# The beginning of a second mixer re-ordered: ScalarE roots, staggered norms, values projected tile by tile, weight splits on GpSimd, the last modulation third moved

## The chip, the cores and the metric

One core of a Trainium2 chip runs the kernel as one program. The metric is the device time of one execution in microseconds (us), the median of several. TensorE (PE) does the matrix products and the transposes, VectorE (DVE), ScalarE (ACT) and GpSimd (POOL) the rest; SyncE (SP) issues most of the transfers. A "slot" is a buffer on the chip that successive tiles of one kind share.

## The reference, cut to what matters

The model has two layers over 256 context and 256 latent tokens (512 tokens, four tiles of 128, width 1024). Each layer is a token mixer and then a mixture of experts, each followed by a residual and a layer norm:

```
for l in range(2):
    sh1, sc1, g1, sh2, sc2, g2 = split(silu(c) @ w_ada[l] + b_ada[l], 6)   # for latents and for context
    h = layer_norm(x) * (1 + sc1) + sh1
    p = h @ w_in[l]          # columns: query down, key/value down, mLSTM q, k, values, output gate, gates, merge gates
    y = (g_a * mla(p) + g_b * mlstm(p)) @ w_out[l]
    x = layer_norm(ALPHA * x + g1 * y, ln1_g[l], ln1_b[l])
    x = layer_norm(ALPHA * x + g2 * hier_moe(modulate(x, sh2, sc2)), ln2_g[l], ln2_b[l])
```

`layer_norm` subtracts the mean and multiplies by `rsqrt(var + 1e-6)`. The mLSTM is a chunked recurrence with gates from 16 columns of `p`; the kernel computes it as masked products over whole tiles, for which the gates' running sums and running maxima are needed first. In the second layer only the latent tokens go on to an output.

## The kernel before

All products are in float32. To keep accuracy with the faster form of float32, an operand is split in a rounded part and a rest: ScalarE copies the rounded part (`split_sb`, L176), and `sub` (L160) subtracts it, on GpSimd every third time and else on VectorE; `mm3` (L192) then does three products for one (L196 to L198).

A planner orders each engine's instructions before the run, by the program's order and its own estimate of when each is ready; on the chip each engine then takes its queue in that order. `issue_after(x)` in the new code puts what a block issues behind the instruction `x` on the engine of `x`. `keep_in_program_order` fixes a transfer in its queue. Generators are woven by hand: `weave(main, steps, fills)` runs one step of `main` and then its share of each filling generator.

The weights of the mixer come through four slots of 128x2048, handed out in halves (`w`, L118); `load_cols` (L438) loads columns of a matrix, `wsplit` (L453) splits them. The shared pools `st` (12 tiles of 128x512), `pm` (4) and `u` (34 in the second layer) hold the rest.

The end of the first layer's experts (`moe`, L1296): the last two pairs of experts are combined into the rows `X[t]` of each tile (`combine`, L1467: a product, L1478 and L1481 on VectorE). Then, tile by tile, come the norm with gains (`stats`, L1487: a square with a sum on ScalarE, L1492, then an inverse root by three Newton steps of VectorE instructions on 128x1, L144 to L154; then L1574 and L1581) and the statistics of the next layer's first norm (again `stats`). After all four tiles the middle third of the second layer's modulation, `ada(1, 1, True)`, is drained: 16 loads of w_ada and 64 matrix instructions (L382). A call `ada(l, g)` does one third g of the six modulation rows of layer l.

The second mixer's begin (`mixer`, L467): `vkr`, the 256 columns for the position key, the gates and half of the key/value down projection, are loaded and split first. Then, for each tile t and each half g of its width, ScalarE writes the normalised half `xn` (L493), TensorE transposes it (L499), ScalarE and VectorE scale and shift (L508, L510), and the result is split into `hTh` and `hTl` (L511, L512). With each half goes a step of `ada(1, 2)`, the last modulation third. Then `tm` (L549) projects each tile on `vkr` (L571), `gates` (L787) makes the gates' sums, maxima and transposes on VectorE while keys and queries are projected (`cm`, L559), the four heads' value columns are loaded, split and projected by `mv_cols` (L594), and the mLSTM is woven with the latent projections (L684). In the first layer, two modulation thirds (1 and 2 of that layer) are woven there as well.

Of the kernel before, what the change touches and what calls it, by code (L numbers as in the profile page):

```python
# [83 lines left out]
class Kern:  # L84
# [77 lines left out]
    def split_sb(self, src, name="s", weights=False):  # L162
# [14 lines left out]
        self.sub(view(lo), src, view(hi).bitcast(F32))  # L177
# [135 lines left out]
    def setup(self):  # L313
# [25 lines left out]
        self.ada_d = [self.dp.tile([2, 6 * D], F32, name=f"ada{l}") for l in range(L)]  # L339
        self.zeros = self.cp.tile([128, 1], F32, name="zeros")  # L340
# [14 lines left out]
    def ada(self, l, g, late=False):  # L355
# [5 lines left out]
        def bias():  # L361
            bt = self.pm(name="bada") if late else (self.u(name="bada") if first else self.w("bada")[:, 0:512])
            for c in range(4):
                a = g * 2048 + c * 512
                (nc.gpsimd if first else nc.sync).dma_start(out=bt[32 * c:32 * c + 32],
                                                            in_=I["b_ada"][l, a:a + 512].partition_broadcast(32))
            return bt
# [85 lines left out]
    def wsplit(self, vs, cols=None):  # L453

        res = []
        for v in vs:
# [10 lines left out]
    def mixer(self, l):  # L467
# [10 lines left out]
        hl = mp.tile([128, 8, 512], F32R, tag="hT", name="hTl", bufs=2)  # L478
        if l == 0:
            xT, xs = [], {}  # L480
            ada0 = self.ada(0, 0)
            next(ada0)
        else:

            vkr = self.load_cols(win, 512, 160, (2208, 96))
            wkr = self.wsplit(vkr)
            ada0 = self.ada(1, 2)
        for t in range(NT):
            r, nb = self.nlx[t] if l else self.ln_scale(self.X[t])
            ts = slice(t * 128, t * 128 + 128)  # L490
            for g in range(2):
                xn = (self.u if l else self.st)(name="xn")
                nc.scalar.activation(xn, self.X[t][:, g * 512:g * 512 + 512], AF.Identity, scale=r, bias=nb)  # L493
# [3 lines left out]
                p = self.ps("t")  # L497
                for k in range(4):
                    nc.tensor.transpose(p[:, k * 128:(k + 1) * 128], xn[:, k * 128:(k + 1) * 128], self.ident)  # L499
# [21 lines left out]
        run(ada0)  # L521
        if l == 0:
# [26 lines left out]
        def tm(v, toks, ws=None):  # L549

            ws = ws or self.wsplit(v)
            n = v[0].shape[2]
            for t in toks:
                p = self.ps("g")
                s = slice(t * 128, t * 128 + 128)
                self.mm3(p[:, 0:n], [(hh[:, k, s], hl[:, k, s], ws[k][0], ws[k][1]) for k in range(8)])
                yield t, p

# [9 lines left out]
        krg = self.sm([128, NT, 48], "krg", bufs=1)  # L568
        kd2 = [self.u(name="kd") for i in range(2)]
        kd = {t: kd2[t // 2][:, (t % 2) * 256:(t % 2) * 256 + 256] for t in range(NT)}  # L570
        for t, p in enumerate(pkr) if l == 0 else tm(vkr, range(NT), wkr):  # L571
            nc.scalar.activation(kd[t][:, 128:256], p[:, 0:128], AF.Copy)
            nc.vector.tensor_copy(krg[:, t], p[:, 128:176])
# [14 lines left out]
        V1 = [mp.tile([128, self.UW], F32, tag="u", name="v1", bufs=self.NU).rearrange("p (a b) -> p a b", a=NT)  # L588
              for h in range(4)]
        tpo = [self.u(name="tpo").rearrange("p (a b) -> p a b", a=4) for h in range(4)]  # L590
        for h in range(4):
            nc.gpsimd.memset(V1[h][:, :, 128:129], 1.0)

        def mv_cols():  # L594
            for c in range(2):
                v = self.load_cols(win, 1184 + c * 256, 256)
                for t, p in tm(v, range(NT)):
                    for i in range(2):
                        nc.scalar.activation(V1[2 * c + i][:, t, 0:128], p[:, i * 128:i * 128 + 128], AF.Copy)  # L599
                    yield  # L600
# [70 lines left out]
        for _ in range(4):  # L671
            next(fill)
# [935 lines left out]
```

## Time and profile before

| | |
|---|---|
| median of 3 runs | 1428.43 us (1427.02 to 1432.36) |
| the profiled execution's own time | 1431.51 us |
| its span, first to last instruction | 1429.4 us |
| busy in the span: TensorE | 1294.4 us (91%) |
| busy: VectorE, ScalarE, GpSimd | 794.9, 451.2, 377.7 us |
| mean granted TensorE clock | 0.947 of full speed |
| read from HBM | 344.62 MB |

Busy time is the time in which an engine has an instruction in work. Matrix products overlap, and their ends are modelled, so that a TensorE which is busy all the time need not be at its peak. The mean over the span mixes stages with different limits, so the seam between the layers has to be read by itself.

### The profile page before, as it was taken

The page shows a single profiled execution, that of the slowest core. Times are in us where ns is not written, and L with a number is a line of the kernel's source. Part 1 is how long each engine was busy: PE and PEld are TensorE (multiplying, and loading weights), DVE is VectorE, ACT ScalarE, POOL GpSimd, SP SyncE. Part 2 cuts the span into 40 slices and gives each one's busy share as a digit, 9 for nine tenths or more (in the row PEclk, how much of TensorE's full clock was granted, in tenths as well). Part 3 has the DMA queues.
Part 4 walks back from the last instruction along what each step waited for, and adds up shares of the span by engine and source line. Part 5 has one row for each costly group of instructions (what it writes and reads, how often), then busy time and mean ns, then how long its engine had stood idle before and what let it go on. Part 6 is the DMA issues. An engine that isn't in the chain of part 4 may idle for free. (4 is left out here: it accounts for less than half of the span.)

```text
span 1429.4 us, 19667 instructions
## 1 busy us (share of the span) xinstructions
PE 1294.4 (91%) x6839; PEld 834.8 (58%) x6839; DVE 794.9 (56%) x2189; ACT 451.2 (32%) x998; POOL 377.7 (26%) x385
## 2 busy tenths in 40 slices
PE   5899999999999828999999959999999749999995
PEld 1788867776776623444454517898878634444342
DVE  3745777553236945555554486478775863343325
ACT  3534344443340102111121137356545212121121
POOL 1310114100343302444343212112524401232222
PEclk9999999999999858989999989999999959999998
DMA  9633464211247567979999968321444768999994
GB/s 326 207 114 131 145 214 140 82 30 59 89 177 269 168 256 250 403 264 409 408 407 409 403 211 278 96 81 39 152 143 132 237 250 329 408 408 406 407 409 158
DMA packets 145970, 339.64 MB, mean 238 GB/s; under 512 B 21552, under 2 KB 67792, under 8 KB 145856
## 3 DMA queue, kind: packets, MB, share of 16 engines
q1 hardware_dynamic: 137184, 322.61, 61.7%
q0 software_dynamic: 6224, 10.31, 2.1%
q10 hardware_dynamic: 2448, 5.31, 1.0%
q8 instruction: 59, 0.97, 0.3%
q14 instruction: 55, 0.45, 0.1%
HBM read 344.62 MB, written 4.29 MB: 244 GB/s over the span
## 5 line engine op out<-in xcount | busy, mean ns | idle before, releaser
L1438 PE MATMUL ps_g<-we,xs 128*64 128x512 f32 x992 | 243.7, 617 | 6.6 <-DMA we<-in_w_e_up 4.2
L1438 PEld LDWEIGHTS ps_g<-we,xs 128*64 128x64 f32 x992 | 76.3, 141 | 148.2 <-issue 141.6
L160 POOL TENSOR_TENSOR wsl<-wc,wsh 128x512 fp32r<-128x512 f32 x54 | 72.5, 1346 | 321.7 <-ACT wsh L176 284.1
L1484 POOL TENSOR_TENSOR X<-X,acc 128x512 f32<-128x512 f32 x96 | 125.2, 1327 | 109.8 <-DVE acc L1478 109.7
L160 DVE TENSOR_TENSOR wsl<-wc,wsh 128x512 fp32r<-128x512 f32 x108 | 84.5, 786 | 98.3 <-ACT wsh L176 87.0
L176 ACT ACTIVATE wsh<-wc 128x512 fp32r<-128x512 f32 x162 | 99.0, 628 | 118.6 <-PE ps_g L197 81.1
L1442 DVE SCALAR_TENSOR_TENSOR si<-si,ws,ps_g 128x256 f32<-128x256 f32 (+1 forms) x33 | 15.8, 480 | 211.4 <-ACT si L1441 211.4
L1461 PE MATMUL ps_a<-we,hidT 128*64 128x512 f32 x496 | 125.3, 595 | 2.1 <-DMA we<-in_w_e_down 1.9
L1394 POOL DMA_INDIRECT xr<-h2d,ti x33 | 34.9, 1057 | 315.2 <-PE ps_t L1406 207.2
L196 PE MATMUL ps_g<-hTh,wsh 128*128 128x512 f32 (+1 forms) x320 | 112.4, 351 | 2.0 <-ACT tg L639 2.0
L197 PE MATMUL ps_g<-hTl,wsh 128*128 128x512 f32 (+1 forms) x320 | 111.1, 347 | 0.0
L198 PE MATMUL ps_g<-hTh,wsl 128*128 128x512 f32 (+1 forms) x320 | 110.6, 346 | 0.0
L196 PE MATMUL ps_g<-wsh,hTh 128*128 128x256 f32 x368 | 105.5, 289 | 2.5 <-ACT v L599 2.4
L197 PE MATMUL ps_g<-wsl,hTh 128*128 128x256 f32 x368 | 104.2, 284 | 0.0
L198 PE MATMUL ps_g<-wsh,hTl 128*128 128x256 f32 x368 | 103.7, 283 | 0.0
L382 PE MATMUL ps_d<-wada,sT 128*32 128x512 f32 x380 | 70.3, 645 | 29.5 <-DMA wada<-in_w_ada 29.4
L1478 DVE TENSOR_TENSOR acc<-ps_d,g 128x512 f32<-128x512 f32 x108 | 74.1, 689 | 38.0 <-PE ps_d L1476 21.9
L1441 ACT ACTIVATE si<-ps_g 128x256 f32<-128x256 f32 (+1 forms) x33 | 12.7, 384 | 245.7 <-PE ps_g L1438 179.0
L1475 PE MATMUL ps_d<-yh,pmr 128*128 128x512 f32 (+1 forms) x200 | 83.7, 419 | 0.4 <-DVE acc L1478 0.2
L1461 PEld LDWEIGHTS ps_a<-we,hidT 128*64 128x64 f32 x496 | 38.6, 137 | 76.1 <-issue 62.8
L1476 PE MATMUL ps_d<-yl,pmr 128*128 128x512 f32 (+1 forms) x200 | 80.2, 403 | 0.9 <-DVE yl L190 0.9
L196 PEld LDWEIGHTS ps_g<-wsh,hTh 128*128 128x128 f32 x368 | 69.6, 190 | 9.2 <-ACT v L599 2.6
(420 smaller groups left out, 2710.3 us busy)
## 6 DMA issues: line engine op xcount, KB each, us to landing
we<-in_w_e_gate SPq DMA_DIRECT2D x124, 512.0 KB
we<-in_w_e_up SPq DMA_DIRECT2D x124, 512.0 KB
we<-in_w_e_down SPq DMA_DIRECT2D x124, 512.0 KB
wada<-in_w_ada SPq DMA_DIRECT2D x95, 512.0 KB
wc<-in_w_in SPq DMA_DIRECT2D x63, 512.0 KB
wc<-in_w_out SPq DMA_DIRECT2D x16, 512.0 KB
wc<-in_w_bo_mla SPq DMA_DIRECT2D x8, 512.0 KB
wc<-in_w_bo_mlstm SPq DMA_DIRECT2D x6, 512.0 KB
```

The costliest lines, as they stand in the source:

```text
L160: eng.tensor_tensor(out=out, in0=a, in1=b, op=OP.subtract)
L176: self.nc.scalar.activation(view(hi), src, AF.Copy)
L196: self.nc.tensor.matmul(out, lhsT=ah, rhs=bh, start=(i == 0), stop=False)
L197: self.nc.tensor.matmul(out, lhsT=ah, rhs=bl, start=False, stop=False)
L198: self.nc.tensor.matmul(out, lhsT=al, rhs=bh, start=False, stop=(i == n - 1))
L382: nc.tensor.matmul(ps[32 * c:32 * c + 32], lhsT=self.sT[:, kb], rhs=wt[c // 2][:, (c % 2) * 512:(c % 2) * 512 + 512], start=(kb == 0), sto ...
L1438: nc.tensor.matmul(p[64 * e:64 * e + 64], lhsT=xs[:, k, 64 * e:64 * e + 64], rhs=W[e, k], start=(k == 0), stop=(k == 7))
L1461: nc.tensor.matmul(p[64 * e:64 * e + 64], lhsT=hT_[:, c, 64 * e:64 * e + 64], rhs=W[e, c, h], start=(c == 0), stop=(c == 1))
L1475: nc.tensor.matmul(p, lhsT=lt, rhs=yh[h][0:m], start=(j == 0), stop=False)
L1476: nc.tensor.matmul(p, lhsT=lt, rhs=yl[h][0:m], start=False, stop=(j == len(parts) - 1))
L1478: nc.vector.tensor_tensor(out=a, in0=p, in1=g2[t // 2][h], op=OP.mult)
L1484: nc.gpsimd.tensor_tensor(out=X, in0=X, in1=a, op=OP.add)
```

## The change

Six things change. The first and the last touch the norms of both layers, the others only the seam between the first layer's experts and the second mixer.

1. `stats` takes the root on ScalarE (`AF.Sqrt` with the scale 1/D and a constant column for epsilon), then VectorE's reciprocal and one Newton step, in place of three Newton steps from an integer guess. It serves the second norm of both layers and the statistics of the next first norm.
2. The norm of a tile becomes a generator with three parts: combination and mean; first norm and the next mean; second statistics. After the experts only the parts (0, 1, 0, 2, 1, 3) by tile are run, the rest at the beginning of the mixer, where each tile starts as soon as its norm is there.
3. In the second layer each tile is projected on `vkr` and on both value matrices right after its start (`from_start`). The values' eight splits are subtracted on GpSimd alone, in tiles from `u`, and their ScalarE copies stand behind tile 0's last copy; the splits of `vkr` stand behind tile 0's last normalised half.
4. Both halves of a tile are normalised and transposed before the first is modulated, and `xn` lies in `st` instead of `u`.
5. The last modulation third, `ada(1, 2)`, is woven with the mLSTM instead.
6. The bias rows of the late modulation third are issued by GpSimd instead of SyncE, and the sums of the norm lie in another small pool.

```diff
-    def split_sb(self, src, name="s", weights=False):
+    def split_sb(self, src, name="s", weights=False, pool=False):
...
         self.nc.scalar.activation(view(hi), src, AF.Copy)
-        self.sub(view(lo), src, view(hi).bitcast(F32))
+        if pool:
+            self.nc.gpsimd.tensor_tensor(out=view(lo), in0=src, in1=view(hi).bitcast(F32), op=OP.subtract)
+        else:
+            self.sub(view(lo), src, view(hi).bitcast(F32))
...
-                (nc.gpsimd if first else nc.sync).dma_start(out=bt[32 * c:32 * c + 32],
+                (nc.gpsimd if late or first else nc.sync).dma_start(out=bt[32 * c:32 * c + 32],
...
-                h, lo = self.split_sb(v[:, k:k + m], "ws", True)
+                h, lo = self.split_sb(v[:, k:k + m], "ws", not far, far)
...
             vkr = self.load_cols(win, 512, 160, (2208, 96))
-            wkr = self.wsplit(vkr)
-            ada0 = self.ada(1, 2)
-        for t in range(NT):
+            krg, kd, kd2 = start_tiles()
+            vv = [self.load_cols(win, 1184 + c * 256, 256) for c in range(2)]
+        def start(t, between=None):
...
-                xn = (self.u if l else self.st)(name="xn")
-                nc.scalar.activation(xn, self.X[t][:, g * 512:g * 512 + 512], AF.Identity, scale=r, bias=nb)
+                xn = self.st(name="xn")
+                done = nc.scalar.activation(xn, self.X[t][:, g * 512:g * 512 + 512], AF.Identity, scale=r, bias=nb)
...
+            if between:
+                with tc.issue_after(done.ins):
+                    between()
+            for g, p in enumerate(pts):
...
-                nc.scalar.activation(oh, h, AF.Copy)
+                done = nc.scalar.activation(oh, h, AF.Copy)
                 self.sub(ol, h, oh.bitcast(F32))
-                next(ada0)
+            return done
+
+        def from_start(t):
+            kr_out(t, next(tm(vkr, [t], wkr))[1])
+            for c in range(2):
+                mv_out(c, t, next(tm(vv[c], [t], wmv[c]))[1])
...
+            wkr, wmv = [], []
+            norm(0)
+            done = start(0, lambda: wkr.extend(self.wsplit(vkr)))
+            norm(2, 1)
+            with tc.issue_after(done.ins):
+                wmv.extend(self.wsplit(v, None, True) for v in vv)
+            start(1)
+            from_start(0)
+            norm(3, 2)
+            start(2)
+            from_start(1)
+            norm(3)
+            start(3)
+            from_start(2)
+            from_start(3)
...
         def mv_cols():
-            for c in range(2):
+            for c in range(0 if l else 2):
...
-        fill2 = self.chain(*[self.ada(0, g) for g in (1, 2)]) if l == 0 else iter(())
+        fill2 = self.chain(*[self.ada(0, g) for g in (1, 2)]) if l == 0 else self.ada(1, 2)
...
-        self.weave(mlstm, 10, [(fill, 32 if last else 34), (fill2, 16)])
+        self.weave(mlstm, 10, [(fill, 32 if last else 34), (fill2, 8 if last else 16)])
...
-            nc.scalar.activation(xrs[xi[0] % 3], X, AF.Square, bias=nm, accum_out=q)
-            nc.vector.tensor_scalar(v, q, 0.5 / D, 0.5 * eps, op0=OP.mult, op1=OP.add)
-            self.newton(r, v, a)
+            junk = self.cp.tile([128, 1024], BF16, tag="st", name="junk", bufs=self.NST)
+            nc.scalar.activation(junk, X, AF.Square, bias=nm, accum_out=q)
+            nc.scalar.activation(r0, q, AF.Sqrt, scale=1.0 / D, bias=self.eps[eps])
+            nc.vector.tensor_scalar(v, q, -0.5 / D, -0.5 * eps, op0=OP.mult, op1=OP.add)
+            nc.vector.reciprocal(r0, r0)
+            nc.vector.tensor_scalar(a, r0, v, r0, op0=OP.mult, op1=OP.mult)
+            nc.vector.scalar_tensor_tensor(r, a, 1.5, r0, op0=OP.add, op1=OP.mult)
...
+        self.norms = {t: norm(t) for t in QT}
+        for t in (2, 2, 3, 3) if last else (0, 1, 0, 2, 1, 3):
+            next(self.norms[t])
```

`kr_out` and `mv_out` write a tile's projection out of TensorE's banks with the instructions that stood at L572, L573 and L599. `start_tiles` hands out the tiles for this, the value tiles with their column of ones among them, earlier than before.

## Rows read from the trace of the kernel before

**Rows 1.** Table by stretches: us, busy per engine (instructions), granted clock, DMA share, GB/s.

```profile
831.50:859.10 27.60, 12.07 (x40) 1.75 (x40) 21.75 (x76) 11.16 (x20) 4.36 (x4) 0.75 0.61 223
...
906.40:916.10 9.70, 7.36 (x49) 7.36 (x50) 4.43 (x12) 3.62 (x10) 1.29 (x1) 0.82 0.14 47
```

**Rows 2.** Groups by form, TensorE, 820 to 932: count, busy, mean ns, idle.

```profile
L196 PE MATMUL ps_g<-wsh,hTh 128*128 128x256 f32 x105 | 30.8, 293 | 2.5 <-ACT v L599 2.4 <-ACT hTh L511 0.2
...
L196 PE MATMUL ps_g<-hTh,wsh 128*128 128x512 f32 x16 | 6.3, 396 | 0.0
...
L196 PE MATMUL ps_g<-hTh,wsh 128*128 128x256 f32 x16 | 4.6, 287 | 0.0
```

**Rows 3.** Timeline, TensorE, 824 to 869: start, us, engine, line, count [idle before].

```profile
824.37 7.07 PE L382 MATMUL ps_d<-wada,sT 128*32 128x512 f32 x64
...
868.00 0.28 PE L196 MATMUL ps_g<-wsh,hTh 128*128 128x256 f32 x1
...
868.12 0.29 PE L197 MATMUL ps_g<-wsl,hTh 128*128 128x256 f32 x1
```

**Rows 4.** Waits of TensorE, 820 to 932: total us, times, longest.

```profile
PE ps_d L382 <- DMA wada<-in_w_ada: 15.0, 5, 11.0
...
PE ps_g L196 <- ACT v L599: 2.4, 1, 2.4
```

**Rows 5.** Waits of all engines, 831 to 880.

```profile
PEld ps_d L382 <- DMA wada<-in_w_ada: 26.6, 12, 11.9
...
ACT xr L1492 <- DVE ln_mv L1584: 23.4, 4, 7.8
```

**Rows 6.** Waits of the sync queue, 790 to 930.

```profile
SPq L378 <- DVE wsl L160: 15.4, 1, 15.4
```

**Rows 7.** Timeline, ScalarE, 822 to 885.

```profile
823.34 1.15 ACT L1492 ACTIVATE xr<-X,ln_mv 128x1024 f32<-128x1024 f32 x1 [6.39 <-DVE ln_mv L1572]
...
841.81 2.17 ACT L176 ACTIVATE wsh<-wc 128x512 fp32r<-128x512 f32 x4
...
858.28 4.32 ACT L493 ACTIVATE xn<-X,ln_nb,ln_r 128x512 f32<-128x512 f32 x6
```

**Rows 8.** Timeline, VectorE, 822 to 885.

```profile
828.72 0.15 DVE L147 TENSOR_SCALAR ln_r<-ln_v 128x1 int32<-128x1 int32 x1
...
830.90 1.28 DVE L1581 SCALAR_TENSOR_TENSOR X<-X,ln_r,ln 128x1024 f32<-128x1024 f32 x1
...
844.41 1.77 DVE L160 TENSOR_TENSOR wsl<-wc,wsh 128x512 fp32r<-128x512 f32 x1
...
846.47 0.68 DVE L160 TENSOR_TENSOR wsl<-wc,wsh 128x512 fp32r<-128x512 f32 x1
```

**Rows 9.** Timeline, ScalarE, 885 to 960.

```profile
885.87 1.28 ACT L800 ACT_TABLE_LOAD   x1
...
917.46 0.20 ACT L857 ACTIVATE em<-ps_t 128x32 f32<-128x32 f32 x1 [0.31 <-DVE uT L856]
```

**Rows 10.** Timeline, GpSimd, 822 to 940.

```profile
842.52 3.11 POOL L160 TENSOR_TENSOR wsl<-wc,wsh 128x512 fp32r<-128x512 f32 x2 [0.78 <-ACT wsh L176]
```

**Rows 11.** Timeline, VectorE, 884 to 935.

```profile
885.89 0.21 DVE L573 COPY krg<-ps_g 128x48 f32<-128x48 f32 x1 [0.18 <-ACT kd L572]
...
917.24 0.19 DVE L856 COPY uT<-ps_t 128x32 f32<-128x32 f32 x1
```

**Rows 12.** Instructions of L382, first layer's mLSTM: duration min/median/max, first and last start.

```profile
L382 PE MATMUL ps_d<-wada,sT x112: 592/592/617, 112.3 to 219.7; 128*32 128x512 f32 x112
```

**Rows 13.** Table by stretches, first layer's mLSTM.

```profile
100.00:200.00 100.00, 100.00 (x705) 77.52 (x704) 65.71 (x241) 45.44 (x140) 12.45 (x9) 1.00 0.49 166
```

**Rows 14.** Timeline, VectorE, the kernel's end.

```profile
1424.61 1.41 DVE L1578 SCALAR_TENSOR_TENSOR X<-X,ln_r,ln 128x512 f32<-128x512 f32 x2
```

**Rows 15.** Table by stretches, before and in the last experts' stage.

```profile
1160.00:1180.00 20.00, 7.18 (x28) 4.12 (x30) 15.32 (x86) 4.61 (x7) 3.01 (x3) 0.50 0.49 190
...
1200.00:1220.00 20.00, 19.70 (x97) 8.45 (x97) 5.81 (x18) 4.64 (x10) 4.49 (x4) 1.00 1.03 408
```

More of the change, by code (lines that the diff above doesn't have):

```diff
@@ L339, in setup @@
         self.ada_d = [self.dp.tile([2, 6 * D], F32, name=f"ada{l}") for l in range(L)]
+        self.eps = {}
+        for e in (EPS, EPS / ALPHA ** 2):
+            self.eps[e] = self.cp.tile([128, 1], F32, name=f"eps{len(self.eps)}")
+            nc.gpsimd.memset(self.eps[e], e)
         self.zeros = self.cp.tile([128, 1], F32, name="zeros")
@@ L510, in mixer, with norm @@
                         nc.vector.tensor_scalar(h[:, k], pv[:, k], sc, sh, op0=OP.mult, op1=OP.add)
-                nc.scalar.activation(oh, h, AF.Copy)
+                done = nc.scalar.activation(oh, h, AF.Copy)
                 self.sub(ol, h, oh.bitcast(F32))
-                next(ada0)
+            return done
[3 more added lines that the diff above has]
+                mv_out(c, t, next(tm(vv[c], [t], wmv[c]))[1])
+        if l == 0:
+            for t in range(NT):
+                start(t)
+        else:
+            def norm(*ts):
+                for t in ts:
+                    next(self.norms[t])
[14 more added lines that the diff above has]
+            from_start(3)
         if l == 0:
@@ L520, in mixer @@
                 nc.scalar.activation(xT[k], p, AF.Copy)
-        run(ada0)
-        if l == 0:
+            run(ada0)
             tc.keep_in_program_order(nc.sync.dma_start(out=self.cst, in_=I["cst"][:, C_CAPF:]))
@@ L565, in cm @@
             return p
[L568 to L573, printed above, removed]
+        if l == 0:
+            krg, kd, kd2 = start_tiles()
+            for t, p in enumerate(pkr):
+                kr_out(t, p)
         gen = self.gates(l, krg[:, :, 32:48])
@@ L587, in mixer @@
                     next(gen)
-        V1 = [mp.tile([128, self.UW], F32, tag="u", name="v1", bufs=self.NU).rearrange("p (a b) -> p a b", a=NT)
-              for h in range(4)]
         tpo = [self.u(name="tpo").rearrange("p (a b) -> p a b", a=4) for h in range(4)]
-        for h in range(4):
-            nc.gpsimd.memset(V1[h][:, :, 128:129], 1.0)
         def mv_cols():
-            for c in range(2):
+            for c in range(0 if l else 2):
                 v = self.load_cols(win, 1184 + c * 256, 256)
                 for t, p in tm(v, range(NT)):
-                    for i in range(2):
-                        nc.scalar.activation(V1[2 * c + i][:, t, 0:128], p[:, i * 128:i * 128 + 128], AF.Copy)
+                    mv_out(c, t, p)
                     yield
@@ L671, in mixer @@
         for _ in range(4):
-            next(fill)
+            next(fill, None)
         gates = next(gen)
@@ L1564, in moe, with norm @@
         self.drain(comb)
-        sums = {t: sm([128, 3], "sum", bufs=n) for t in QT}
+        sums = {t: self.ss_tile([128, 2, 6], "st")[:, 0] for t in QT}
         comb = combine(done, sums)
-        for t in QT:
+        def norm(t):
             for h in range(2):
@@ L1587, in moe @@
             self.nlx[t] = (r, nb)
+            yield
+        self.norms = {t: norm(t) for t in QT}
+        for t in (2, 2, 3, 3) if last else (0, 1, 0, 2, 1, 3):
+            next(self.norms[t])
         if not last:
```

50 lines of the change are left out of this document (34 added, 16 removed).

## The prediction, made before the changed kernel had run

> **What bounds the kernel now.** The kernel's two layers are a mixer and a mixture of experts each, and the change sits at the seam between the first layer's experts and the second mixer, plus the last norm of the kernel. So I read the views of that seam. First the table by stretches, for TensorE [rows 1]: it is busy for 12.07 of the 27.6 us from 831.5, where the experts' last product and the middle modulation third are through, and even that at a clock of 0.75. I take the seam to end at 932, with the second mLSTM in full swing: 100.5 us. How much of that is work? The groups by form hold 105 records of the 128x256 product's first line; its two sister lines have 104 each, and the same form with the operands the other way round has 16 in each of three lines, 361 in all; the 128x512 form has three groups of 16 [rows 2]. Back to back a 128x256 product starts 0.12 us after the one before [rows 3], so 361 are 43 us; 48 of twice the width, at twice that (an estimate), 11.5 us; the last modulation third is 64 instructions, which took 7.07 us when its sister third ran undisturbed [rows 3]; some 48 transposes and small products at about 0.12 us, 6 us. That is 67 to 68 us of work. **TensorE loses 33 us here**, and this is all that a rearrangement of the seam can win.
>
> Next, who makes it wait. TensorE's own list names the modulation's weights for 15.0 us, one wait of 11.0 in it, and the evacuation of a value projection for 2.4 [rows 4]; on the weight loader's own count the same cause makes 26.6 us [rows 5]. But the load was late only because its slot was: the sync queue stood 15.4 us before that load, until VectorE's last split of the first w_in columns (key and gate columns) [rows 6]. And that split was late because ScalarE takes its instructions in order: it waited 23.4 us for the norms' means [rows 5], did the splits at 841.81 and the first normalised tile only at 858.28, behind the last tile's squares [rows 7], though tile 0's normalised rows were there when the instruction at 830.90 had run [rows 8] plus one more statistic. Tile 0 waits for tile 3; that is the seam's chain.
>
> **The change part by part.** The profiled execution took 1431.51 us, a span of 1429.4 and 2.1 around it; the median of the three runs is 1428.43, 3.1 less. The terms below come from that execution and are microseconds saved against its own time; the result is then carried to the median.
>
> *Roots on ScalarE.* Eight small VectorE steps per statistic become four, and one root. Tile 0's first Newton chain runs from 828.72 to 830.90 with other work between [rows 8], about 0.3 a step, so three dependent steps are 0.9 and the root 0.20, as the small exponential is [rows 9]: a saving of about 1 per statistic on the chain. Against it stands a function table, 1.28 for the one load that this trace shows beside an exponential [rows 9]; squares, copies and identities ran on the tables of either neighbour without a load. One load at the seam, one at the end. The Trainium skill (ScalarE: Activation LUTs, What ACT_TABLE_LOAD costs) puts a switch to another set at 2.66 us with its drain; the row shows the load's 1.28 and no drain, and by the page the two places would cost 2.8 more together, 1419.3.
>
> *Staggered norms.* Tile 0 no longer waits for tile 3. From its first square at 823.34, 1.25 long with the read [rows 7]: load 1.28, root and steps 1.1, the affine row 1.28, mean 0.15, giving 828.4; the second square, root, steps and shift 2.5, giving 830.9; two normalised halves at 0.72 (six in 4.32 [rows 7]), giving 832.3; transposes, modulation, copy and subtract, about 3.4 by their chain's pieces, giving 836. VectorE is full then, with evictions and tile 1's norm before this in its queue: up to 5 later. I take 839: TensorE waits 7 (4.5 to 9.5) from 831.5, less its transposes.
>
> *Clock after the wait.* In the stretch 906.4 to 916.1, after a wait of 2.4, the granted clock was 0.82 of the full 2.4 GHz, and in 831.5 to 859.1, with its long waits, 0.75, so part of the time at 1.2 [rows 1]. 0.18 of 9.7 is 1.7; two such dips are 3.5 (1.7 to 6.9, the latter 0.25 of 27.6).
>
> *Values per tile, splits on GpSimd.* A tile now feeds three projections of 24 products, 2.9 each. The two value weights need eight splits on GpSimd, 3.11 for two [rows 10], so 12.4 after the first copy, and four of them, 6.2, before any value product. They queue behind tile 0, so from about 837 to 850. Tile 0's and 1's key projections (5.8) and tile 0's first value projection (2.9) fill in; the rest, 3.7, is waited out: I take 4 (0 to 9.5, where only tile 0's key projection is there to fill).
>
> *VectorE beside GpSimd.* The same subtract took 1.77 while GpSimd's ran and 0.68 after [rows 8, 10], 1.09 more. Eight times that is 8.7 on VectorE, which has some 20 of work left then; TensorE is 7 or so behind it with queued projections, so most is hidden. I take 2 (0 to 8.7). The Trainium skill (SBUF — State Buffer, Who interferes with whom) calls this an exclusive lock: a VectorE instruction with two SBUF inputs waits out a GpSimd one that reads SBUF. The trace agrees, with 1.77 against 0.68; by the rule in full, with every split costing VectorE its whole length, the term would be 12.4 and the time 1426.9, which the first rival below takes in.
>
> *The gates' cover.* From the last key and gate columns at 885.89 to the transposed gates at 917.24 are 31 us [rows 11], a VectorE chain that TensorE fills with query, key and value projections; the values are now used up before. What is left: one tile's values 5.8, keys 11.5, queries 5.8, together 23. Unless the latent projections are pulled ahead, 8 is uncovered: I take 4 (0 to 8).
>
> *The last modulation third in the mLSTM.* Its 64 instructions count as work in either place. The first layer weaves two thirds through its own mLSTM, 112 instructions from 112.3 to 219.7 [rows 12], and there TensorE was busy 100 of 100 us [rows 13]. I take 2 for slots and queue (0 to 15.0, what TensorE waited for these loads at the seam [rows 4]). At the seam the sync queue now carries only the six halves of the first projections; key columns behind them wait for a slot that the first splits free, long before need. The bias rows moved to GpSimd's queue stand ahead of its splits and cost under 1.5, hidden behind tile 0.
>
> **Sum.** 33 less (7 + 3.5 + 4 + 2 + 4 + 2 = 22.5) is 10.5. At the end of the kernel VectorE ends its last norm at 1426.0 (1424.61 and 1.41) [rows 14]; two tiles spare eight steps, some 3, and pay one table load: 1.5 (0.3 to 2.5). Together 12. It should carry through: 1160 to 1180, before the last experts, the weight queues are half idle (0.49), and the 408 GB/s stream that bounds the rest is full only later [rows 15]; its slots come free with the mixer, so it starts earlier with it. Result: 1431.5 - 12 = 1419.5 us for an execution like the profiled one, and 3.1 less for the median, **1416.5 us**.
>
> **The rivals.**
> *GpSimd's splits set the seam's pace.* Value projections wait 9.5 in place of 4 and VectorE pays 8.7 in place of 2: 12.2 less saved, 1428.7. For it: GpSimd's row and the doubled subtract. Against: VectorE's slack.
> *The gates' chain lies bare.* 8 in place of 4: 1420.5; for it the wait of 2.4 there already [rows 4].
> *Slower: the mLSTM waits for the woven third.* The sync queue is in order; one load before an occupied slot holds every projection's weights behind it. At the seam such waits came to 26.6 on the loader [rows 5]. That in place of 2 gives 1441; past 21 of waiting the result is more than 0.5% slower, past 14 the gain is gone. For it: 15.4 of queue wait for one slot [rows 6]. Against: the first layer's full TensorE [rows 13].
> *It does not carry.* If the expert weights' stream has its own start, only the end's 1.5 stays: 1427. Against: the half-idle queues [rows 15].
>
> **How the numbers follow.** Forecast 0.57, GpSimd 0.14, gates 0.10, slower 0.09, not carried 0.10. A measurement here tells 0.5%, 7.1 us, from no change. The forecast's own range, its waits all small or two of them large, is 1406 to 1422. The 8-in-10 range reaches over the gates and to GpSimd and the case that does not carry: 1406 to 1430. Faster by over 0.5% (under 1421.3) holds most of the forecast and half of the gates' case: 0.60; within, 0.28; slower, 0.12.
>
> **What would show it.** Tile 0's normalised halves near 833 and its first key product near 839; no modulation products between 831 and 880; one table load of 1.28 before the first root; GpSimd's eight subtracts in a row; last key columns near 870 to 875 and the mLSTM's first weights near 905 in place of 918. Wrong would be: roots with a load each, TensorE waiting for GpSimd past 850, weight loads of the woven third ahead of waiting projections, or an experts' stage that starts no earlier.

## The result, and the profile after

The changed kernel takes 1446.94 us (median of 4 runs, 1442.79 to 1449.05) beside 1428.36 for the kernel before on the same chip: 1.0117 times as long, 95% interval 1.0095 to 1.0138. Forecast were 1416.5 and a range of 1406 to 1430. The profiled execution took 1445.77 us, its span 1444.0 beside 1429.4, so 14.6 longer. Three places in the two traces divide this difference: the second mixer's last projection, as VectorE scales it ("yo"), the first gather of the experts (GpSimd, "xr"), and the end.

The kernel before, timelines of VectorE and GpSimd:

```profile
1135.11 0.68 DVE L748 SCALAR_TENSOR_TENSOR yo<-ps_g,g 128x512 f32<-128x512 f32 x1
...
1170.67 1.14 POOL L1394 DMA_INDIRECT xr<-h2d,ti  x1 [32.29 <-DVE ws L1428]
```

The changed kernel, the same:

```profile
1145.35 0.68 DVE L801 SCALAR_TENSOR_TENSOR yo<-ps_g,g 128x512 f32<-128x512 f32 x1
...
1186.61 1.14 POOL L1447 DMA_INDIRECT xr<-h2d,ti  x1 [38.00 <-DVE ws L1481]
```

| stretch | before | after | difference |
|---|---|---|---|
| start to the last projection | 1135.1 | 1145.4 | +10.2 |
| from there to the first gather | 35.6 | 41.3 | +5.7 |
| from there to the end | 258.7 | 257.4 | -1.3 |

Forecast were 10.5 less in the first, no change in the second and 1.5 less in the third (the roots at the kernel's end).

Executions do not reach the seam at the same moment: the middle third, whose 64 records open it on TensorE, starts at 824.37 before, at 823.34 after, and between 817.75 and 826.88 in the runs below. So lengths are counted from its start as well. Table by stretches, from there to the last key and gate columns and on to the last projection, in the kernel before:

```profile
824.37:885.89 61.52, 44.52 (x274) 22.75 (x274) 44.72 (x133) 31.75 (x64) 11.28 (x12) 0.89 0.76 257
885.89:1135.11 249.22, 243.52 (x1658) 209.92 (x1656) 170.60 (x456) 118.79 (x286) 79.02 (x100) 0.99 0.39 122
```

and in the changed kernel, where most value projections lie in the first of the two:

```profile
823.34:894.79 71.45, 49.06 (x358) 40.13 (x358) 41.21 (x100) 41.27 (x92) 23.82 (x25) 0.86 0.41 123
894.79:1145.35 250.56, 244.09 (x1575) 196.34 (x1573) 165.20 (x453) 110.79 (x267) 76.95 (x95) 0.99 0.47 149
```

Together 310.7 and 322.0 us: 11.3 longer. The same two programs, traced a second time (e3 and e2 below), took 311.0 and 326.4, so a single trace of the changed kernel can be 4 us off.

The seam first. The changed kernel's table by stretches, as [rows 1], with the whole stretch from 831.5 to 932 behind it:

```profile
831.50:859.10 27.60, 10.46 (x61) 9.43 (x62) 21.22 (x53) 20.69 (x42) 10.57 (x9) 0.69 0.57 176
906.40:916.10 9.70, 9.70 (x56) 7.77 (x55) 3.25 (x7) 3.44 (x7) 2.59 (x3) 1.00 0.36 108
831.50:932.00 100.50, 79.20 (x535) 69.71 (x536) 49.78 (x128) 46.47 (x105) 25.75 (x21) 0.90 0.40 126
```

and that whole stretch in the kernel before:

```profile
831.50:932.00 100.50, 81.20 (x521) 61.83 (x522) 63.03 (x176) 49.89 (x108) 18.52 (x21) 0.92 0.56 189
```

In the stretch from 831.5 to 859.1 TensorE is no busier than before (10.46 us against 12.07), and over the whole it idles 21.3 us beside 19.3. Its waits there, as [rows 4], are of another kind:

```profile
PE ps_t L537 <- DVE h L552: 9.3, 1, 9.3
PE ps_t L537 <- ACT xn L531: 5.9, 1, 5.9
PE ps_g L200 <- POOL wsl L178: 3.6, 3, 1.7
PE ps_g L199 <- ACT v L512: 1.8, 1, 1.8
```

The modulation's weights are gone from the list; tile 0's own modulation (h) holds it now. ScalarE's timeline says why, as [rows 7]:

```profile
837.41 1.65 ACT L176 ACTIVATE wsh<-wc 128x512 fp32r<-128x512 f32 x3
838.97 1.13 ACT L1545 ACTIVATE junk<-X,ln_mv 128x1024 bf16<-128x1024 f32 x1
...
840.10 1.13 ACT L1545 ACTIVATE junk<-X,ln_mv 128x1024 bf16<-128x1024 f32 x1
...
844.46 1.52 ACT L531 ACTIVATE xn<-X,ln_nb,ln_r 128x512 f32<-128x512 f32 x2 [2.77 <-DVE ln_nb L1647]
845.89 0.78 ACT L550 ACTIVATE h<-ps_t,ss 128x128 f32<-128x128 f32 x2
```

Tile 0 is transposed by 838.3, but two squares of other tiles and tile 1's normalised halves (with a wait of 2.77) stand ahead of its modulation. TensorE's timeline, with the moved third, as [rows 3, 12]:

```profile
836.33 1.97 PE L537 MATMUL ps_t<-ident,xn 128*128 128x128 f32 x8 [5.92 <-ACT xn L531]
847.58 1.09 PE L537 MATMUL ps_t<-ident,xn 128*128 128x128 f32 x4 [9.28 <-DVE h L552]
...
850.71 0.56 PE L199 MATMUL ps_g<-wsh,hTh 128*128 128x256 f32 x1
...
876.61 1.04 PE L389 MATMUL ps_d<-wada,sT 128*32 128x512 f32 x2
...
949.89 1.05 PE L389 MATMUL ps_d<-wada,sT 128*32 128x512 f32 x4
950.88 0.70 PE L946 MATMUL ps_a<-mqk 64*128 64x256 f32 x2
951.50 1.05 PE L389 MATMUL ps_d<-wada,sT 128*32 128x512 f32 x4
```

Two things are to be seen. The first key product comes at 850.71, not 839. And the third's 64 records (two for each of its 32 products) stand in small groups, 16 in all from 876.6 to 995.3, mostly of two or four, and a group of two takes as long as one of four: 1.04 and 1.05 on the record, 0.97 to 0.99 to the next product (949.89 to 950.88). 16 of them are 15.7 us, where 64 in a row took 7.07 [rows 3]. Each of these products fills 32 of the 128 columns (128*32 in the rows), and four with different columns run at once only if they stand side by side.

### The profile page after: what moved, and what is told of

Read it like the earlier page. It is cut to its first block, busy times and chain, and to the rows that moved or that the text cites. A ratio compares the mean times of both kernels' runs of the same rounds, so it can differ in the third digit from the quotient of the medians.

```text
span 1444.0 us, 19627 instructions
## 1 busy us (share of the span) xinstructions
PE 1297.8 (90%) x6839; PEld 837.5 (58%) x6839; DVE 786.2 (54%) x2144; ACT 454.5 (31%) x1010; POOL 388.2 (27%) x396
## 5 line engine op out<-in xcount | busy, mean ns | idle before, releaser
L1491 PE MATMUL ps_g<-we,xs 128*64 128x512 f32 x992 | 239.3, 607 | 6.2 <-DMA we<-in_w_e_up 3.9
L160 POOL TENSOR_TENSOR wsl<-wc,wsh 128x512 fp32r<-128x512 f32 x52 | 69.3, 1335 | 342.3 <-ACT wsh L176 316.5
L160 DVE TENSOR_TENSOR wsl<-wc,wsh 128x512 fp32r<-128x512 f32 x102 | 81.5, 805 | 110.6 <-ACT wsh L176 99.6
## 6 DMA issues: line engine op xcount, KB each, us to landing
we<-in_w_e_gate SPq DMA_DIRECT2D x124, 512.0 KB, 10.2
```

The costliest lines, as they stand in the source:

```text
L160: eng.tensor_tensor(out=out, in0=a, in1=b, op=OP.subtract)
L1491: nc.tensor.matmul(p[64 * e:64 * e + 64], lhsT=xs[:, k, 64 * e:64 * e + 64], rhs=W[e, k], start=(k == 0), stop=(k == 7))
```

## The experiments

Theories. M: the moved third costs its scattered groups in full, since TensorE has no idle time in the mLSTM. G: the gates come late (the last key and gate columns at 894.8, before 885.9 [rows 11]; the mLSTM's first weights at 933.0, before 918.6) and leave the mLSTM bare. Q: ScalarE's order holds tile 0. S, later C: the 5.7 us behind the last projection come from the place of a buffer, or from writes on ScalarE's queue. All times are medians with the kernel before on the same chip; its medians were 1428.1 to 1430.9.

### The moved third: e1, e4, e8, e17, e18

**e1**, the changed kernel:

```diff
-                nc.tensor.matmul(ps[32 * c:32 * c + 32], lhsT=self.sT[:, kb], ...)
+                mm = nc.tensor.matmul(ps[32 * c:32 * c + 32], lhsT=self.sT[:, kb], ...)
+                if (l, g) == (1, 2):
+                    self.tc.keep_in_program_order(mm)
```

> The changed kernel, with the 32 modulation matmuls of the moved third held in program order on TensorE, so that they stand in 8 groups of four and not scattered in 16 groups. Theory M (the scattered third): in the trace of the changed kernel a group takes 0.97 us whether it holds one, two or four of these 32-column matmuls, 16 groups 15.5 us against 7.07 us for all in a row in the kernel before; 8 groups should take 7.8 us, so 7 to 8 us come back: about 1439 us. Theory G (late gates): the loss in the mLSTM comes from its start 14.4 us later, with its chain bare; the grouping changes that by nothing: 1445 to 1448. Theory S (slots) expects no change either.

Measured: 1438.42, ratio 1.0055 (1.004 to 1.007); M's number. From the middle third to the last projection it is 315.2 us, in the changed kernel 322.0. Timeline of TensorE in e1, eight records in the time that two took above:

```profile
944.04 1.07 PE L389 MATMUL ps_d<-wada,sT 128*32 128x512 f32 x8
945.04 0.71 PE L989 MATMUL ps_a<-v,mw 128*128 128x129 f32 x4
```

The Trainium skill (TensorE: Matmul & The Clock Gate, Why this matters for your kernels) says that products with few output columns run concurrently when each lands in a column group of its own; the rows agree, and show the other side, that one standing alone takes as long as four together.

**e4**, the changed kernel with the third back at the seam:

```diff
+            ada0 = self.ada(1, 2)          # one next(ada0) behind each tile, run(ada0) after the last
-        fill2 = ... if l == 0 else self.ada(1, 2)
+        fill2 = ... if l == 0 else iter(())
```

> The changed kernel, with the modulation third back at the second mixer's begin, one step behind each tile, and not in the mLSTM. Theory M: its matmuls fall where TensorE waits anyway (9.3 us for tile 0's modulation, 5.9 us for a normalized half in the changed kernel), so most of the 15.5 us is covered: 6 to 10 us faster than the changed kernel, 1437 to 1441, unless the loads of this third (it waited 15.0 us for them in the kernel before) hold TensorE again. Theory G: the gates and the mLSTM start as late as in the changed kernel, 1445 to 1450.

Measured: 1439.18, ratio 1.0062 (1.0043 to 1.0082). As M has it: 313.0 us from the middle third to the last projection, 9 less than in the changed kernel.

**e8**, the kernel before with only the third moved, and woven at the changed kernel's pace:

```diff
-            ada0 = self.ada(1, 2)
+            ada0 = iter(())
-        fill2 = ... if l == 0 else iter(())
+        fill2 = ... if l == 0 else self.ada(1, 2)
```

> The kernel before, with the last modulation third moved from the second mixer's begin into its mLSTM as in the change, and nothing else of it. By the prediction's reading TensorE waits 15.0 us for this third's weights at the seam, and moving it should give up to that back. Theory M: there the third only fills waits that the norms make anyway (ScalarE stood 23.4 us for their means), and in the mLSTM it stands in about 13 groups of 0.97 us on a TensorE that has no idle time: 5 to 13 us slower, 1436 to 1444.

Measured: 1445.76, ratio 1.0107 (1.0084 to 1.0131): a little past M's end. This one edit makes nearly as large a loss as the whole change. Its trace is of the fastest of its four executions (1440.87), which reached the seam 6.5 us before the kernel before did. Table by stretches, cut as above:

```profile
817.91:879.88 61.97, 29.32 (x210) 22.68 (x210) 43.21 (x132) 31.76 (x64) 10.49 (x10) 0.72 0.38 114
879.88:1145.12 265.24, 258.39 (x1722) 210.36 (x1720) 173.90 (x458) 119.25 (x286) 80.89 (x102) 1.00 0.46 147
```

Up to the last key and gate columns nothing is saved (61.97 us against 61.52), though TensorE is busy 15 us less there; behind them it is 16.0 longer (265.24 against 249.22). From the last projection on it takes no longer than the kernel before.

**e17 and e18**, the changed kernel and the one before, each with

```diff
-            for c in range(4):
+            for c in range(0 if (l, g) == (1, 2) and kb else 4):
```

> The changed kernel with seven eighths of the last modulation third's products left out (its first four of 32 stay; every load of its weights stays), so that the second output norm's scale and the experts' gate are not the reference's and the routing differs: only the time to the last projection of the second mixer is compared (1145.4 us in the changed kernel, 1135.1 in the kernel before). Theory M: on a TensorE without idle time the 16 scattered groups of 0.98 us cost their whole 15.7 us, 14 or so of them in the part left out: the last projection near 1131 to 1133. If the third's price in the mLSTM lay in slots and queues, its loads being kept, most of it stays: 1140 or later.

> The kernel before with the same products left out, and its loads kept. Theory M: at the seam the third stands in the waits for the norms and costs little more than these waits: the last projection between 1129 and 1135 us (1135.1 in the kernel before), against 12 us or more that the same products cost in the changed kernel. If the third costs the same in both places, as the prediction had it but for 2 us, it comes near 1123 to 1125.

Both leave out products that the result needs; their times stand for one execution each. The last projection in e17:

```profile
1135.27 0.68 DVE L801 SCALAR_TENSOR_TENSOR yo<-ps_g,g 128x512 f32<-128x512 f32 x1
```

and in e18:

```profile
1135.66 0.67 DVE L748 SCALAR_TENSOR_TENSOR yo<-ps_g,g 128x512 f32<-128x512 f32 x1
```

From the middle third these are 311.8 and 308.8 us. So seven eighths of the products cost 10.2 us in the changed kernel (10.1 between the two positions, 1145.35 less 1135.27), some 2 to 4 less than M expected, and 2.0 in the kernel before, where a price that is the same in both places would be 10 to 12. The loads were there in both. The third's products are thus nearly the whole 11.3 us; and without them, the rest of the change has gained nothing (311.8 against 310.7).

What stood in their place at the seam, in e18, on TensorE and in the table by stretches:

```profile
861.65 1.97 PE L499 MATMUL ps_t<-ident,xn 128*128 128x128 f32 x8 [21.55 <-ACT xn L493]
```

```profile
826.88:887.41 60.53, 32.24 (x218) 22.76 (x218) 43.09 (x133) 31.46 (x64) 11.20 (x12) 0.75 0.76 261
887.41:1135.66 248.25, 241.92 (x1658) 208.34 (x1656) 170.62 (x456) 118.78 (x286) 78.94 (x100) 1.00 0.40 122
```

Without the products TensorE waits 21.55 us for the normalised halves, which come as long after the norms' first square as before (34.95 us, there 34.94). But its granted clock is 0.75 in this stretch, 0.89 with the products in place, so it is at 1.2 GHz for longer. Part of what the products free may be lost to that; no run separates the two. The same holds for e8 (0.72).

### The order at the seam: e6, e7, e11, e12, e16

**e6**, on e1:

```diff
-            norm(2, 1)
             with tc.issue_after(done.ins):
+                norm(2, 1)
                 wmv.extend(self.wsplit(v, None, True) for v in vv)
-            start(1)
+                start(1)
```

> The pinned kernel of e1, with the norms and normalized halves of tiles 1 and 2 queued on ScalarE behind tile 0's modulation (six instructions that stood in the changed kernel behind two squares, two roots and tile 1's normalized halves, which waited 2.77 us). Theory Q (ScalarE's order): tile 0 is modulated near 839 to 843 and not 845.9 to 850, its first key product comes near 844 and not 850.7, TensorE's wait of 9.3 us shrinks to about 2, and 4 to 7 us of it reach the end: 1432 to 1435. Rival: VectorE and the norm of tile 1 set the pace, tile 1 comes later by what tile 0 gains and the wait moves there: 1437 to 1440.

Measured: 1435.43, ratio 1.0029 (1.0015 to 1.0043), 0.26% less than e1. Timeline of TensorE in e6:

```profile
836.80 1.97 PE L539 MATMUL ps_t<-ident,xn 128*128 128x128 f32 x8 [5.93 <-ACT xn L533]
843.62 0.58 PE L199 MATMUL ps_g<-wsh,hTh 128*128 128x256 f32 x1 [4.85 <-ACT hTh L555]
```

The first key product is 7.1 earlier than in the changed kernel, some 4 us of it reach the end. From the middle third to the last projection it is 309.3 us, 1.5 less than in the kernel before, with the third still in the mLSTM. What the third takes there is 3.3 by e1 against e17 (315.2 and 311.8), or 8.8 by its eight groups' own time in e6: the seam itself then gives some 5 to 10 (an estimate).

**e7**, the kernel before with the changed `stats` alone (square root on ScalarE, one correction step):

> The kernel before, with the statistics' reciprocal root taken from a square root on ScalarE and one correction step on VectorE, as in the change, and nothing else of it. By the prediction's terms a statistic is 1 us shorter and a place pays one table load of 1.28: between 1 and 3 us faster, 1428 to 1430 beside a kernel before of about 1431. If roots between squares, copies and identities brought a table load each, four more at the seam: 5 us slower.

Measured: 1429.06, ratio 0.9987 (0.9968 to 1.0006). In line, but not told from no change.

**e11 and e12.** e11 is e4 with the edits of e6 and e9 (below); e12 also takes the values out of `from_start` and projects them in `mv_cols`, behind keys and queries:

```diff
-            for c in range(2):
-                mv_out(c, t, next(tm(vv[c], [t], wmv[c]))[1])
```

> The kernel of e4 (everything of the change, but the third at the seam), with tile 0's modulation first as in e6 and the writes behind the evictions as in e9. If the gains add: 1439.2 less 3 to 4 (e6 against e1) less 5 (e9) is 1430 to 1431. Theory M holds the third free of charge only while TensorE has idle time at the seam; with tile 0's modulation first there is less of that, and the sum would be some us higher.

> The kernel of e11, with the value projections traced behind the key and gate columns of all four tiles and behind the queries and keys, where the kernel before has them (the splits stay on GpSimd, queued as in the change). Theory G (late gates): in e4 the last key and gate columns came at 898.9 us against 885.9 before and the first mLSTM weights at 933.7 against 918.6, and TensorE lost 8 us from 932 to 960 against 2.1; with the keys first the gates start 10 us earlier, the values fill their chain again, and 4 to 6 us come: 1425. If late gates cost nothing, as e1 suggests (its mLSTM starts 7.6 us late and ends 1.3 us late), no change against e11.

Measured: e11 1437.09, ratio 1.0052 (1.0033 to 1.007); e12 1431.63, ratio 1.0023 (1.0004 to 1.0041). e11 misses its sum by 6 to 7; 5 of these are the move of the writes, which gave nothing in e9 either. That the third fills the same idle time which tile 0's earlier start takes away would explain the rest, but is only argued. e12's 4 us (0.29%, the intervals still touch) speak for G where the third is at the seam; TensorE's waits in e12, 820 to 1000, show what is left:

```profile
PE ps_d L390 <- DMA wada<-in_w_ada: 15.0, 6, 7.1
PE ps_t L538 <- ACT xn L532: 5.9, 1, 5.9
```

The wait for the third's weights is back at its old 15.0 [rows 4].

**e16**, on e14 (below), the value weights' subtractions shared between VectorE and GpSimd:

```diff
-                h, lo = self.split_sb(v[:, k:k + m], "ws", not far, far)
+                h, lo = self.split_sb(v[:, k:k + m], "ws", not far)
```

> The kernel of e14 with the eight subtractions of the value weights' splits shared out as all others are, two on VectorE to one on GpSimd, and not all on GpSimd. The prediction's first rival (GpSimd's splits set the pace and hold VectorE, 1.77 against 0.68 us for a subtract beside one): if it holds, 3 to 8 us faster than e14; if the splits are covered, no change.

Measured: 1431.24, ratio 1.0 (0.9987 to 1.0012) beside e14's 0.9997: no change. The splits on GpSimd are covered there, where the values come behind keys and queries; for the changed kernel's own order this was not tried.

### Behind the last projection: e2, e3, e5, e9, e10, e13 to e15

**e2 and e3.**

```diff
         def load_rows():
+            for _ in range(8 if last else 0):      # e3: 26, in the kernel before
+                self.u(name="pad")
```

> The changed kernel, with eight unused buffers of the work pool taken in the second layer just before the rows of the first output norm (gain, bias, gate), so that these rows lie in the same of the 34 buffers as in the kernel before (the change took eight normalized halves out of this pool). Theory S: the shift of eight is what makes the first expert weights wait 4.8 us for a VectorE norm step, land among the write of a normalized tile (8.5 us to landing instead of 3.4) and hold ScalarE's queue (two issues over 7.55 us instead of 1.97), so that the logits come 5.6 us later; with the shift undone about 5.6 us come back: 1441. Theories M and G: none of this is on the path or caused by the slots: 1446 to 1448.

> The kernel before, with 26 unused buffers taken at the same place: 26 of 34 is the shift of minus eight that the change makes, and nothing else of the change is there. Theory S: 5 to 6 us slower than before, 1434, with the same wait of the first expert weights and the same stuck issue on ScalarE. Otherwise 1428, as before.

Measured: e2 1451.05, ratio 1.0133 (1.0098 to 1.0169); e3 1430.64, ratio 1.0007 (0.9993 to 1.0022). A buffer that nothing uses takes no place: the addresses of the built programs are those of the kernels that they were made from. They test nothing, and serve as repeats of both kernels. In e2's trace the last projection is at 1152.88, 7.5 later than in the changed kernel's: the seam was reached 3.1 later, and the rest took 4.4 longer at a mean granted clock of 0.94 in place of 0.96.

**e5**, on e1, gives the rows another pool:

```diff
-            rows["g"] = self.rows_of(I["ln1_g"][l], "lg", self.u)
+            new = self.st if last else self.u
+            rows["g"] = self.rows_of(I["ln1_g"][l], "lg", new)     # "b" too
```

> The pinned kernel of e1, with the second layer's two gain rows and two bias rows of the output norm loaded into the pool that holds the normalized tiles, not into the mixer's work pool. Unused buffers took no place, so e2 and e3 left every buffer where it was and say nothing of theory S. In the changed kernel's memory the first expert-weight buffer behind the four of the weight pool lies over the second half of the gain row, last read by VectorE at 1149.1 us; in the kernel before it lies over a gate row, free 4.8 us earlier. Theory S: with the rows elsewhere the weights are issued right behind the expert gate rows, the write of the first normalized tile lands in about 3.4 us again, ScalarE's second pair of issues takes about 2 us instead of 7.5, the logits come 5 to 6 us earlier: 1433. If the logits come earlier and the end does not, the experts' stream sets the end. Other theories: no change, 1438.

Measured: 1441.42, ratio 1.0084 (1.0056 to 1.0113), no gain. The weights were issued earlier, as S has it, and ScalarE then stood at the first pair of writes:

```profile
1150.06 2.92 ACTq L817 DMA_DIRECT2D h2d<-h  x2
1153.38 1.08 ACT L266 ACTIVATE h2T<-ps_t 128x512 f32<-128x512 f32 x2 [35.91 <-DMA we<-in_w_e_down]
```

So S falls as it was put. In the built program SP's loads and ScalarE's writes take eight completion counters in turn, and a transfer waits until the one before it on its counter has landed; in the traces it is an expert load ("we") that ends ScalarE's wait. ScalarE in the changed kernel, at the second pair of writes, the last of which has the counter of the expert load issued at 1161.67:

```profile
1160.96 7.55 ACTq L814 DMA_DIRECT2D h2d<-h  x2
1168.62 1.08 ACT L266 ACTIVATE h2T<-ps_a 128x512 f32<-128x512 f32 x2 [13.33 <-DMA we<-in_w_e_up]
```

and in the kernel before:

```profile
1150.64 1.97 ACTq L761 DMA_DIRECT2D h2d<-h  x2
1152.71 1.09 ACT L263 ACTIVATE h2T<-ps_a 128x512 f32<-128x512 f32 x2 [7.67 <-PE ps_a L261]
```

**e9 and e10**, e6 and the kernel before with these writes behind the logits' evictions:

```diff
+        if last:
+            with tc.issue_after(ev.ins):           # ev: the last eviction of the transposes
+                for t in QT:
+                    write(t)
```

> The kernel of e6 (pinned third, tile 0's modulation first), with the second layer's four writes of normalized halves issued on ScalarE behind all four evictions of the logits' transposes, not between them. What e5 showed: with the gain rows out of the way the first weights were issued at once, and ScalarE then stood 6.2 us at the write of the first normalized tile, so the slot is not the cause by itself. In the program SP's weight loads and ScalarE's writes take eight completion counters in turn, and a transfer waits until the one before it on its counter has landed: in the changed kernel the last write has the counter of an expert load issued 0.7 us after that write's data is there, in the kernel before that of a load issued 4 us before. Theory C (counters): with the writes behind the evictions nothing of the logits waits for an expert load, the evictions follow TensorE by under 1 us and the logits come 5 us earlier than in e6 by the interval from the last projection (26.6 us there, 21 to 22 here): 1430 to 1431 beside 1435.4. If the end does not follow, the experts' stream sets it: 1435.

> The kernel before with the same move of the four writes. Theory C: here ScalarE stood only about 2 us at its second pair of writes, so 1 to 2 us at most: 1429 to 1431 beside 1430.7.

Measured: e9 1434.08, ratio 1.0025 (1.0006 to 1.0043); e10 1432.24, ratio 1.002 (1.0004 to 1.0036), slower by 0.2%. The logits come 5.6 earlier in e9, the gather does not: the wait has moved ahead of the routing's exponential. ScalarE in e9:

```profile
1154.31 7.30 ACTq L821 DMA_DIRECT2D h2d<-h  x4
1161.66 0.21 ACT L1272 ACTIVATE rex<-rd 128x8 f32<-128x8 f32 x1 [10.65 <-DMA we<-in_w_e_up]
```

**e13**, the changed kernel with nothing but

```diff
-                    nc.scalar.dma_start(out=self.h2_d[l][...], in_=self.h2[t][g])
+                    (nc.gpsimd if last else nc.scalar).dma_start(out=self.h2_d[l][...], in_=self.h2[t][g])
```

> The changed kernel, with the second layer's writes of normalized halves issued by GpSimd and not by ScalarE, and nothing else. In e9 the logits came 5.6 us earlier after the last projection (21.0 instead of 26.6) and the first gather did not (41.7 against 40.3), since ScalarE now stood 7.3 us at the writes in front of the routing's next exponential. Theory C (counters on ScalarE's queue): with the writes on a queue of which the routing needs nothing, from the last projection to the first gather it takes about 35 us as in the kernel before (35.6; 41.3 in the changed kernel), and 4 to 6 us reach the end: 1441 to 1443. Rival: the experts' weight stream, issued 4.8 us late for its buffer, sets the end: no change, 1446 to 1448.

Measured: 1442.88, ratio 1.0091 (1.0073 to 1.011) against 1.0117. VectorE and GpSimd in e13:

```profile
1145.19 0.67 DVE L801 SCALAR_TENSOR_TENSOR yo<-ps_g,g 128x512 f32<-128x512 f32 x1
...
1180.24 1.09 POOL L1447 DMA_INDIRECT xr<-h2d,ti  x1 [17.74 <-DVE ws L1481]
```

From the last projection to the first gather it is 35.1 us again, while the first weights behind the gate rows are issued as late as in the changed kernel (1150.37, there 1150.54); the fifth load is no longer held (1152.17, there 1161.09). C holds by this trace; the medians lean the same way, but their intervals touch.

**e14 and e15**: e12 without its writes behind the evictions, and e7, each with e13's edit.

> The kernel of e12 (staggered norms and ScalarE roots as in the change, third at the seam, tile 0's modulation first, values behind keys and queries) with the writes issued by GpSimd. Theory C: e12 had 38.7 us from the last projection to the first gather, 35 should be left, so about 3 us: 1428 to 1429 beside a kernel before of 1430.5. If the writes were hidden there: 1431 to 1432.

> The kernel before with the roots on ScalarE (e7: 0.9987 of the time before) and the writes issued by GpSimd. Here ScalarE stood 2.0 us at its second pair of writes, so theory C gives at most 1 to 2 us more: 1427 to 1429, a ratio of 0.997 to 0.999; without it 0.999.

Measured: e14 1429.87, ratio 0.9997 (0.9981 to 1.0013); e15 1428.74, ratio 0.9993 (0.9979 to 1.0007). e14 wins back the whole loss, and neither is told from the kernel before. No version beat it, so the gain that was forecast was not found in any order tried.

## Why the prediction was wrong, point by point

- **"Its 64 instructions count as work in either place", "I take 2" for the third in the mLSTM: the step that failed.** With the third's 7 us counted as work at the seam and in the mLSTM alike, moving it had a net price of 2. But at the seam its products stood in a wait that the norms make (e18: 2.0 us less without seven eighths of them, with 21.55 us of bare wait instead), and in the mLSTM, where TensorE has no idle time to speak of (243.52 of 249.22 us busy in the kernel before), the same products cost 10.2 us (e17). The row of the first layer's full TensorE [rows 13] was read as a sign that nothing waits there; it meant also that every product added there is paid. In the changed kernel it was paid in groups of two and four (e1: some 8 us of it). e8 shows the edit by itself: 15 us by the medians, 16.0 behind the gate columns by its trace.
- **"TensorE loses 33 us here": the rest of the gain did not come.** Without the third's products the changed kernel is still 1.1 longer to the last projection than the kernel before (e17), not 10.5 shorter. Of the 33 us, TensorE idled 19.3; in the others it was busy, for part of them at the lower clock (0.92 in the mean). The changed seam idles as long (21.3) at 0.90, which is 10 us of full speed in 100.5 where the clock's term had 3.5; how much of that falls into waits is not separated. Two causes follow, each worth some 4 us (the second shown only with the third at the seam); the remainder is open.
- **"TensorE waits 7": mis-sized.** Tile 0's halves came at 835.47, forecast near 833; the first key product at 850.71, forecast 839. The sum had the modulation follow the transposes and put VectorE's queue at up to 5, but not ScalarE's, where the order put tile 1's norm first. e6 gives 3 to 4 us back.
- **The gates' chain.** First mLSTM weights at 933.0, forecast 905: not 4 us of bare chain, but late keys of tile 3 and transposes queued behind keys and queries (the gates' rows were ready at 899.5, their transposes began at 913.95). What this costs in the changed kernel is not settled: e12 gives 4 us for it with the third at the seam; e17, without the third's products, is as late in the gates (last columns 894.9), and from there to the last projection it is 8.8 shorter than the kernel before, which has its value projections still to do there.
- **"It should carry through": wrong by 5.7.** That the weight queues are half idle [rows 15] said nothing of a write on ScalarE's queue that waits for an expert load on its counter (e13).
- **Right.** No modulation products between 831 and 876; one table load of 1.28 ahead of the first root, at 823.57; TensorE's waits for GpSimd 3.6, forecast 4, so that the first rival's 9.5 did not come (its price on VectorE was tried only in e14's order, e16). The end of the kernel, 1.3 shorter beside 1.5 forecast, is near by luck: from the last norms' first square to VectorE's end it is 8.45 us before and 7.58 after, and in e7 too, so the roots give 0.9 there; from the first gather to the end the runs spread from 257.2 to 258.9. The rival on the other side, the mLSTM waiting for the woven third, was the right edit with another mechanism: TensorE waited for none of the third's loads.

## What to carry to other kernels

Work that fills a wait is nearly free only there: before it is moved, ask what TensorE would do in its place, and price it in full wherever the engine is busy throughout. Compare stretches from a common point of the two programs, not from the start: here the seam was reached up to 9 us apart. Narrow products that run four at a time must stay side by side; a planner that drops them singly into gaps makes each cost what four cost. A transfer issued from a computing engine's queue can hold that engine until some other queue's transfer has landed, as ScalarE's writes did here, so look at what stands behind it.

## What the runs showed of the hardware that was not expected

A 32-column product of 512 took 1.04 us on the record for two records, 1.05 for four and 1.07 for eight, which is 0.97 to 1.00 to the next product. With seven eighths of the third's products left out at the seam, the granted clock from the middle third to the last gate columns was 0.75 in place of 0.89, with a wait of 21.55 us in it. The roots cost one table load of 1.28 at the seam among squares, copies and identities, and the squares right before and behind it showed no further load.
